# The experts of the first 16 tokens by fetched rows, the dense expert products over the other 240 tokens

## The chip, the core and the metric

The kernel runs on one NeuronCore of a Trainium2 chip. The core has TensorE (matrix products into PSUM), VectorE, ScalarE, GpSimd and SyncE, which run side by side, each through its own list of instructions in order, and wait for each other by semaphores; 16 DMA engines move data between HBM and the core's SBUF. The metric is the device time of one execution in microseconds, the median of several runs.

## The reference

A network of two layers over 256 tokens of 1024 channels, followed by a second block of another kind, all in float32. The change is in PEER, the layer of experts, which each of the two layers has. Each of 8 heads of a token picks the 16 best of 16,384 experts through two sets of 128 sub-keys; the picked experts are rows of two tables, `u_emb` and `v_emb`:

```python
q = jnp.einsum('td,dhk->thk', x_t, w_q).reshape(T, PEER_HEADS, 2, PEER_HALF)
s = jnp.einsum('thpk,hpnk->thpn', q, sub_keys).astype(jnp.float32)
sv, si = lax.top_k(s, K)
cand = (sv[:, :, 0, :, None] + sv[:, :, 1, None, :]).reshape(T, PEER_HEADS, K * K)
cidx = (si[:, :, 0, :, None] * PEER_NKEYS + si[:, :, 1, None, :]).reshape(T, PEER_HEADS, K * K)
fv, fpos = lax.top_k(cand, K)
eidx = jnp.take_along_axis(cidx, fpos, axis=-1)
gate = jax.nn.softmax(fv, axis=-1)
u = u_emb[eidx]
v = v_emb[eidx]
act = jax.nn.gelu(jnp.einsum('thkd,td->thk', u, x_t).astype(jnp.float32), approximate=False)
return jnp.einsum('thk,thkd->td', (gate * act).astype(x_t.dtype), v)
```

## The kernel before

The kernel doesn't gather. `peer` computes every expert for every token, densely: U h for all 16,384 experts, gelu, times the gate, which is zero for those not picked, and then the product with V. Both tables are streamed from HBM in 128 tiles of 128 experts (512 KB each) per layer.

All large products are made in three parts: each operand is split into a high and a low float32r part, and the product is high x high, high x low and low x high (`mm3`, and the loop in `product`). A float32r matmul is one record in the trace, a product of plain float32 is two. A tile of weights is loaded by SyncE's queue into `raw` (three places), its high part `whi` is made by ScalarE (line 88) and its low part `wlo` by VectorE (line 95), both with three places; `Stream` holds this order, and keeps three tiles split ahead of the one in use.

`peer` goes through these stages:

- Queries and scores, then **U**: for each of 128 tiles `lin_t("ut", hT)` makes one block of 128 experts by 256 tokens in 8 x 3 matmuls (line 364). The tokens `hh`, `hl` are the moving operand, so a matmul has 256 columns. During the first 64 tiles (`I0`) `Background` lets VectorE do the routing (`peer_top`, `peer_route`) in pieces: after each tile a budget of 1,450 ns of it is written into the order (`pump`), by an estimate for each piece.
- During the second 64 tiles the gates are spread by expert, in groups of four tokens: VectorE makes one-hot tiles `pm`, `qm`, ScalarE multiplies the gates in (line 967), TensorE multiplies the two (line 974), and VectorE multiplies the result into the activations `wl`, `wu` (`gates`). 64 groups cover the tokens.
- **V**: for each of 128 tiles the activations of its experts are split (`split_w`, two tiles ahead, line 984 on ScalarE, 985 on VectorE) and multiplied: 8 blocks of 128 channels by 256 tokens, three matmuls each (lines 303 to 305), summed in four PSUM banks `pss`. In layer 0, 56 steps of the modulation run beside V on VectorE (line 214), each with a load of 512 KB into one of three `sp` places.
- `turn_over` adds the result to x and makes the next stage's operand.

GpSimd has nothing to do in V. The order on every engine is the order of the Python calls; each engine waits only for the data and the places of its next instruction.

Of the kernel before, what the change touches and what calls it, by code (L numbers as in the profile page):

```python
# [43 lines left out]
class Stream:  # L44
    """Weights in the order of their use: loads and splits into two float32r parts run ahead."""
# [46 lines left out]
    def end(self):  # L92
        """The low part."""
# [26 lines left out]
class Slots:  # L120
    """A ring of given places."""
# [9 lines left out]
class Background:  # L131
    """Work that is traced between the products, by its time on VectorE."""
# [28 lines left out]
def net(ctx, tc, A, out):  # L161
# [37 lines left out]

    consts = cst.tile([128, 2], FT, name="consts")  # L200
# [17 lines left out]
    def ada_done(l, i):  # L218
        """Finish the modulation vector i of layer l: add its bias."""
# [5 lines left out]
    def ada_gain(l, i, norm):  # L225
        """(1 + scale) * gain, by channel."""
# [5 lines left out]
    def spread_row(g, dst):  # L232
        """A vector by channel [128, 8] as a row on every partition."""
# [11 lines left out]
    def gains(name):  # L245
        """Scale and shift by channel behind a norm."""
# [24 lines left out]
    def mix(main, side):  # L271
        """Spread side evenly among main, from its start."""
# [1765 lines left out]
```

## Time and profile before

| | |
|---|---|
| runs | 2477.17, 2473.5, 2476.11 us |
| median | 2476.11 us |
| profiled execution, first to last instruction | 2471.6 us |
| TensorE busy | 2416.0 us, 98% |
| VectorE busy | 1849.0 us, 75% |
| ScalarE busy | 1383.7 us, 56% |
| GpSimd busy | 18.2 us, 1% |
| U of layer 0, first to last matmul | about 168 to 590 us |
| V of layer 0 | about 592 to 955 us |
| U and V of layer 1 | about 1187 to 1609 and 1610 to 1973 us |

The profile names an instruction by its line, its engine and the tiles that it writes and reads (`pa<-gh,whi`: the accumulator `pa` from `gh` and `whi`), with partitions x elements. TensorE's matmuls overlap in the trace, so the length of a record (0.28 us for 256 columns) is not the time that it costs; the distance from one start to the next is. "PEclk" is the granted clock as a share of 2.4 GHz. A row of the timeline with "x16" is 16 records in a row, its length from the first's start to the last's end. Idle time stands behind its row in brackets with what ended it.

### The profile page before, as it was taken

How to read it: one execution, taken by the hardware profiler on the slowest of the kernel's cores; microseconds unless marked ns; L12 is line 12 of the kernel's file. 1: busy time of each engine (PE TensorE's matmuls, PEld its weight loads, DVE VectorE, ACT ScalarE, POOL GpSimd, SP SyncE). 2: the span in 40 equal slices, each digit the busy share in tenths (PEclk: the TensorE clock that was granted, in tenths of full speed). 3: DMA queues.
4: the chain of work that ended last, by engine and by line, in shares of the span. 5: the costliest groups of instructions: out<-in, count | busy, mean ns of one | idle time of the engine just before them, and what ended most of it. 6: DMA issues, size and time to landing. Idle time of an engine off the chain costs nothing. (4 is left out here: it accounts for less than half of the span.)

```text
span 2471.6 us, 49525 instructions
## 1 busy us (share of the span) xinstructions
PE 2416.0 (98%) x19700; PEld 2368.7 (96%) x19700; DVE 1849.0 (75%) x3537; ACT 1383.7 (56%) x2666; POOL 18.2 (1%) x31
## 2 busy tenths in 40 slices
PE   5999999999999999999999999999999999999998
PEld 4899999999999999889999999999999988999998
DVE  7988988897777778777888888855555676476864
ACT  4565467775454446666455777654444564455443
POOL 0000000000000000000000000000000000000000
PEclk8999999999999999999999999999999999999999
DMA  9555554446777776445555444455665552034564
GB/s 380 232 183 180 188 172 138 134 138 205 269 270 269 269 270 210 154 146 195 172 185 183 150 133 137 154 183 186 187 187 184 176 176 72 26 120 158 186 194 137
DMA packets 123640, 450.23 MB, mean 182 GB/s; under 512 B 14136, under 2 KB 15160, under 8 KB 122256
## 3 DMA queue, kind: packets, MB, share of 16 engines
q1 hardware_dynamic: 122320, 439.53, 53.4%
q0 software_dynamic: 1088, 7.54, 0.8%
q8 instruction: 154, 2.52, 0.4%
q14 instruction: 78, 0.64, 0.1%
HBM read 443.87 MB, written 3.15 MB: 181 GB/s over the span
## 5 line engine op out<-in xcount | busy, mean ns | idle before, releaser
L95 DVE TENSOR_TENSOR wlo<-raw,whi 128x1024 fp32r<-128x1024 f32 x701 | 854.4, 1220 | 253.1 <-ACT whi L88 249.9
L364 PE MATMUL pa<-hh,whi 128*128 128x256 f32 (+1 forms) x2904 | 826.1, 286 | 0.0
L364 PE MATMUL pa<-hl,whi 128*128 128x256 f32 (+1 forms) x2904 | 807.5, 281 | 0.0
L364 PE MATMUL pa<-hh,wlo 128*128 128x256 f32 (+1 forms) x2904 | 804.0, 282 | 0.9 <-DVE wlo L95 0.9
L88 ACT ACTIVATE whi<-raw 128x1024 fp32r<-128x1024 f32 x701 | 735.2, 1050 | 95.4 <-PE pa L304 50.7
L304 PE MATMUL pa<-gl,whi 128*128 128x256 f32 x2000 | 561.9, 281 | 0.0
L305 PE MATMUL pa<-gh,wlo 128*128 128x256 f32 x2000 | 561.9, 281 | 0.0
L303 PE MATMUL pa<-gh,whi 128*128 128x256 f32 x2000 | 561.9, 281 | 0.0
L364 PEld LDWEIGHTS pa<-hh,whi 128*128 128x128 f32 x2904 | 546.9, 188 | 2.4 <-issue 1.3
L364 PEld LDWEIGHTS pa<-hl,whi 128*128 128x128 f32 x2904 | 545.8, 189 | 1.0 <-DVE hl L575 0.8
L364 PEld LDWEIGHTS pa<-hh,wlo 128*128 128x128 f32 x2904 | 542.8, 189 | 1.4 <-DVE wlo L95 1.3
L303 PEld LDWEIGHTS pa<-gh,whi 128*128 128x128 f32 x2000 | 376.9, 188 | 0.0
L305 PEld LDWEIGHTS pa<-gh,wlo 128*128 128x128 f32 x2000 | 376.9, 188 | 0.0
L304 PEld LDWEIGHTS pa<-gl,whi 128*128 128x128 f32 x2000 | 376.8, 188 | 0.0
L967 ACT ACTIVATE qm<-qm,wij 128x128 f32<-128x128 f32 x512 | 163.9, 402 | 26.1 <-DVE qm L959 25.6
L984 ACT ACTIVATE gh<-wu 128x256 fp32r<-128x256 f32 x128 | 53.4, 417 | 181.1 <-PE pa L305 181.0
L984 ACT ACTIVATE gh<-wl 128x256 fp32r<-128x256 f32 x126 | 52.4, 417 | 174.9 <-PE pa L305 174.0
L946 ACT ACTIVATE wl<-pa 128x256 f32<-128x256 f32 x128 | 49.1, 383 | 152.0 <-PE pa L364 151.8
L974 PE MATMUL pb<-qm,pm 128*128 128x128 f32 x1024 | 132.4, 275 | 0.0
L974 PEld LDWEIGHTS pb<-qm,pm 128*128 128x128 f32 x1024 | 123.8, 191 | 0.0
L957 DVE TENSOR_TENSOR pm<-iota,wij 128x512 f32<-128x512 f32 x128 | 87.4, 683 | 43.8 <-PE pb L974 43.8
L985 DVE TENSOR_TENSOR gl<-wu,gh 128x256 fp32r<-128x256 f32 x128 | 54.4, 425 | 67.7 <-ACT gh L984 64.1
(546 smaller groups left out, 3107.1 us busy)
## 6 DMA issues: line engine op xcount, KB each, us to landing
raw<-in_ut_dram SPq DMA_DIRECT2D x256, 512.0 KB, 3.5
raw<-in_v_dram SPq DMA_DIRECT2D x256, 512.0 KB, 4.1
sp<-in_ada_dram SPq DMA_DIRECT2D x56, 512.0 KB, 4.8
ada<-in_ada_dram SPq DMA_DIRECT2D x40, 512.0 KB, 10.2
raw<-in_peer_q_dram SPq DMA_DIRECT2D x32, 512.0 KB, 3.9
raw<-in_up_dram SPq DMA_DIRECT2D x32, 512.0 KB, 3.6
raw<-in_down_dram SPq DMA_DIRECT2D x32, 512.0 KB, 3.5
raw<-in_od_in_dram SPq DMA_DIRECT2D x24, 512.0 KB, 4.2
```

The costliest lines, as they stand in the source:

```text
L88: self.nc.scalar.activation(hi[:, :width], t[:, :width], AF.Copy)
L95: self.nc.vector.tensor_tensor(lo, t, hi, op=OP.subtract)
L303: PE.matmul(ps, lhsT=lh, rhs=rh, start=start, stop=False)
L304: PE.matmul(ps, lhsT=lh, rhs=rl, start=False, stop=False)
L305: PE.matmul(ps, lhsT=ll, rhs=rh, start=False, stop=stop)
L364: PE.matmul(ps, lhsT=part[a], rhs=part[b], start=start and i == 0, stop=stop and i == len(names) - 1)
L946: ACT.activation(t[:, k, gtok:], ps[:, gtok:], AF.Gelu)
L957: V.tensor_tensor(pm, iota[:, None, :].to_broadcast([128, 4, 128]), wij[:, 2, t0:t0 + 4, None].to_broadcast([128, 4, 128]), op=OP.is_equal)
L967: ACT.activation(qm[:, j], qm[:, j], AF.Copy, scale=wij[:, 0, t:t + 1])
L974: PE.matmul(ps[:, j * 128:j * 128 + 128], lhsT=pm[:, j], rhs=qm[:, j], start=True, stop=True)
L984: ACT.activation(gh, t[:, k], AF.Copy)
L985: V.tensor_tensor(gl, t[:, k], gh, op=OP.subtract)
```

## The change

The first 16 tokens (`SP`) leave the dense products. Their picks are 16 tokens x 8 heads x 16 = 2,048 rows of each table; with token and head on the 128 partitions that is 16 picks per partition. `peer_route` packs gate and expert number of these tokens into `pk`, and eight small transfers on GpSimd's queue bring them to `picks` (128 partitions, 16 gates and 16 numbers). The dense U, the one-hot groups, the gates and the dense V then cover 240 tokens (`ND`), 60 groups instead of 64.

Between U and V, ScalarE copies the identity and the first 16 tokens' operand (`reps`, both parts, repeated for the 8 heads), and 16 matmuls bring these onto the partitions in two PSUM banks `htok`. The generator `sparse` does the rest beside V: 16 indirect transfers of 128 rows of 4 KB from U (512 KB each) by GpSimd, VectorE's product of each with `htok` with a sum in two halves of 512, a gelu, the gate, then 16 such transfers from V and a multiply-add each into `ysp`. It holds two places for rows in layer 0 and five in layer 1. From the fourth V tile on, each tile's budget is 450 ns in layer 0 and 900 in layer 1; a row counts 1,300. At the end 8 matmuls of 16 columns with `folds` add the heads' sums to the 16 columns of `pss` that the dense product leaves out. The modulation steps of layer 0 have two places instead of three.

```diff
+SP = 16
+ND = S - SP
@@ product
+        ps = acc(hT.w - hT.c0)[:n]
+            part = {"lh": w[0][:, cs], "ll": w[1][:, cs], "rh": hT.hh[:, k, hT.c0:hT.w],
+                    "rl": hT.hl[:, k, hT.c0:hT.w]}
@@ into
+        mm3(block(pss, c)[:, c0:], w[0][:, cs], w[1][:, cs], rh, rl, start and c % 2 == 0, stop and c % 2 == 1)
@@ peer_route
+        if b == 0:
+            pk = pool.tile([128, 8, 2, 16], FT, name="pk")
+            V.tensor_copy(pk[:SP, :, 0], gate[:SP])
+            V.scalar_tensor_tensor(pk[:SP, :, 1], sel[:SP, 0], 128.0, sel[:SP, 1], op0=OP.mult, op1=OP.add)
+            for h in range(8):
+                G.dma_start(picks[h * SP:h * SP + SP], pk[:SP, h])
@@ peer, between U and V
+            htok = [bank(), bank()]
+            identr = two.tile([128, 128], FR, name="identr")
+            ACT.activation(identr, ident, AF.Copy)
+            reps = [two.tile([128, 8, 8, SP], FR, name="reps", tag="rows", bufs=2) for _ in range(2)]
+            for rep, t in zip(reps, (hT.hh, hT.hl)):
+                ACT.activation(rep, t[:, :, None, :SP].to_broadcast([128, 8, 8, SP]), AF.Copy)
+            for k in range(8):
+                for n, rep in enumerate(reps):
+                    PE.matmul(htok[k // 4][:, k % 4 * 128:k % 4 * 128 + 128],
+                              lhsT=rep[:, k].rearrange("p h t -> p (h t)"), rhs=identr, start=n == 0, stop=n == 1)
...
+                pools["spare"] = (Slots(places[1:]), 2)
...
+            def sparse():
+                pick = two.tile([128, 16], I32, name="pick")
+                act = two.tile([128, 16], FT, name="act")
+                V.tensor_scalar(pick, picks[:, 1], float(l * 16384), None, op0=OP.add)
+                def fetch(table, k):
+                    r = rows.tile(None, FT, "rows")
+                    G.indirect_dma_start(out=r, out_offset=None, in_=A[table].rearrange("l i p d -> (l i p) d"),
+                                         in_offset=bass.IndirectOffsetOnAxis(ap=pick[:, k:k + 1], axis=0))
+                    return r
+                order = [(t, k) for t in ("u", "v") for k in range(16)]
+                ahead = len(rows.places)
+                got = [fetch(*o) for o in order[:ahead]]
+                yield 300
+                for n, (t, k) in enumerate(order):
+                    r = got.pop(0)
+                    if t == "u":
+                        hs = (slice(0, 512), slice(512, 1024))
+                        for q in range(2):
+                            V.tensor_tensor_reduce(r[:, hs[q]], r[:, hs[q]], htok[q], scale=1.0,
+                                                   scalar=act[:, k:k + 1] if q else 0.0, op0=OP.mult, op1=OP.add,
+                                                   accum_out=act[:, k:k + 1])
+                    elif k == 0:
+                        ACT.activation(act, act, AF.Gelu)
+                        V.tensor_tensor(act, act, picks[:, 0], op=OP.mult)
+                        V.tensor_scalar(ysp, r, act[:, 0:1], None, op0=OP.mult)
+                    else:
+                        V.scalar_tensor_tensor(ysp, r, act[:, k:k + 1], ysp, op0=OP.mult, op1=OP.add)
+                    if n + ahead < 32:
+                        got.append(fetch(*order[n + ahead]))
+                    yield 1300
+                for c in range(8):
+                    PE.matmul(block(pss, c)[:, :SP], lhsT=ysp[:, c * 128:c * 128 + 128], rhs=folds, start=False, stop=False)
+                yield 0
+            bg.set(sparse())
@@ the loop over V's tiles
+                if i == 120:
+                    bg.flush()
+                if i > 2:
+                    bg.pump(450 if l == 0 else 900)
                 split_w(i + 2)
                 w_ = st.next("v")
```

Two places in the order. The first is ScalarE between U and V of layer 0; `gtmp` is the gelu of U's last tiles, `wij_r` and `gh` are the high parts of the first experts' activations. Before:

```order
L88 ACTIVATE whi<-raw 128x1024
L984 ACTIVATE wij_r<-wl 128x256
L949 ACTIVATE gtmp<-pa 128x256
L984 ACTIVATE gh<-wl 128x256
L240 ACTIVATE sp<-pb 128x512 x2
L984 ACTIVATE gh<-wl 128x256
L88 ACTIVATE whi<-raw 128x1024
```

And now:

```order
L90 ACTIVATE whi<-raw 128x1024
L998 ACTIVATE wij_r<-wl 128x240
L963 ACTIVATE gtmp<-pa 128x240
L998 ACTIVATE gh<-wl 128x240
L1080 ACTIVATE identr<-ident 128x128
L1083 ACTIVATE reps<-hh 128x1024
L1083 ACTIVATE reps<-hl 128x1024
L243 ACTIVATE sp<-pb 128x512 x2
L998 ACTIVATE gh<-wl 128x240
L90 ACTIVATE whi<-raw 128x1024
```

The three copies stand behind the first `gh`. On TensorE the 16 matmuls that read them stand right behind U's last matmul, ahead of V's first.

The second place is VectorE at V's first tiles in layer 0; the line pairs `L985`/`L999` and `L95`/`L97` are the low parts of the activations and of the weights, `L214`/`L217` a modulation step. Before:

```order
L985 TENSOR_TENSOR gl<-wl,gh 128x256
L95 TENSOR_TENSOR wlo<-raw,whi 128x1024
L985 TENSOR_TENSOR gl<-wl,gh 128x256
L95 TENSOR_TENSOR wlo<-raw,whi 128x1024
L985 TENSOR_TENSOR gl<-wl,gh 128x256
L214 ISA sp,mod<-sp 128x1024
L214 ISA mod 128x1
L95 TENSOR_TENSOR wlo<-raw,whi 128x1024
```

And now:

```order
L999 TENSOR_TENSOR gl<-wl,gh 128x240
L97 TENSOR_TENSOR wlo<-raw,whi 128x1024
L1103 TENSOR_SCALAR pick<-picks 128x16
L1120 ISA rows,act<-rows,pb 128x512
L1120 ISA act 128x1
L1120 ISA rows,act<-rows,pb,act 128x512
L1120 ISA act 128x1
L999 TENSOR_TENSOR gl<-wl,gh 128x240
L217 ISA sp,mod<-sp 128x1024
L217 ISA mod 128x1
L97 TENSOR_TENSOR wlo<-raw,whi 128x1024
```

The row numbers (`pick`) and the first fetched row's product stand directly one behind the other, ahead of the next tile's `gl` and `wlo`. Later rows of the order have one such row in every third tile of layer 0.

## Rows read from the trace of the kernel before

**Rows 1.** The page: span, and its part 1, busy time by engine.

```profile
span 2471.6 us, 49525 instructions
PE 2416.0 (98%) x19700; PEld 2368.7 (96%) x19700; DVE 1849.0 (75%) x3537; ACT 1383.7 (56%) x2666; POOL 18.2 (1%) x31
```

**Rows 2.** Busy time by stretch: two of U in layer 0, V in layers 0 and 1.

```profile
core 0: us, PE busy (x) PEld busy (x) DVE busy (x) ACT busy (x) POOL busy (x), PEclk, DMA share, GB/s
230.00:300.00 70.00, 70.00 (x592) 70.00 (x591) 64.37 (x188) 35.97 (x55) 0.00 (x0) 1.00 0.60 189
250.00:350.00 100.00, 100.00 (x844) 100.00 (x843) 88.40 (x263) 53.46 (x78) 0.00 (x0) 1.00 0.58 186
700.00:800.00 100.00, 100.00 (x847) 100.00 (x847) 74.70 (x103) 48.38 (x72) 0.00 (x0) 1.00 0.76 270
1700.00:1800.00 100.00, 100.00 (x848) 100.00 (x847) 58.19 (x71) 47.91 (x70) 0.00 (x0) 1.00 0.61 186
```

**Rows 3.** Timeline of TensorE elsewhere: start us, length us, engine, line, operation, tiles, forms.

```profile
1080.57 0.39 PE L305 MATMUL pa<-whi,ml 128*128 128x512 f32 x1
1080.80 0.39 PE L303 MATMUL pa<-whi,mh 128*128 128x512 f32 x1
...
2068.23 0.28 PE L364 MATMUL pa<-hl,whi 128*32 128x256 f32 x1
2068.35 0.28 PE L364 MATMUL pa<-hh,wlo 128*32 128x256 f32 x1
...
2162.95 1.89 PE L1735 MATMUL pb<-rhs,XT 128*128 128x64 f32 x16
...
2234.07 1.89 PE L1800 MATMUL pb<-kT,qT 128*128 128x256 f32 x8
```

**Rows 4.** The page's part 5, groups: busy us, mean ns | idle before.

```profile
L95 DVE TENSOR_TENSOR wlo<-raw,whi 128x1024 fp32r<-128x1024 f32 x701 | 854.4, 1220 | 253.1 <-ACT whi L88 249.9
L88 ACT ACTIVATE whi<-raw 128x1024 fp32r<-128x1024 f32 x701 | 735.2, 1050 | 95.4 <-PE pa L304 50.7
L967 ACT ACTIVATE qm<-qm,wij 128x128 f32<-128x128 f32 x512 | 163.9, 402 | 26.1 <-DVE qm L959 25.6
L974 PE MATMUL pb<-qm,pm 128*128 128x128 f32 x1024 | 132.4, 275 | 0.0
L957 DVE TENSOR_TENSOR pm<-iota,wij 128x512 f32<-128x512 f32 x128 | 87.4, 683 | 43.8 <-PE pb L974 43.8
L985 DVE TENSOR_TENSOR gl<-wu,gh 128x256 fp32r<-128x256 f32 x128 | 54.4, 425 | 67.7 <-ACT gh L984 64.1
```

**Rows 5.** Timeline from U to V in layer 0.

```profile
590.11 0.28 PE L364 MATMUL pa<-hh,wlo 128*128 128x256 f32 x1
590.22 1.95 PE L237 MATMUL pb<-ident,csil 128*128 128x128 f32 x16
590.42 0.38 ACT L949 ACTIVATE gtmp<-pa 128x256 f32<-128x256 f32 x1 [1.21 <-PE pa L364]
...
591.29 0.42 ACT L984 ACTIVATE gh<-wl 128x256 fp32r<-128x256 f32 x1 [0.49 <-DVE wu L950]
```

**Rows 6.** Groups of VectorE in V of layer 0, 600 to 950.

```profile
L214 DVE CUSTOM_DVE_ANT_0 sp<-sp 128x1024 f32<-128x1024 f32 x56 | 68.3, 1219 | 0.0
```

**Rows 7.** Waits in V of layer 0, 600 to 950: total us, times, longest.

```profile
ACT gh L984 <- PE pa L305: 172.9, 118, 1.5
```

**Rows 8.** Stretches around the idle time at 82 us; columns as in rows 2.

```profile
82.00:87.00 5.00, 1.50 (x6) 0.59 (x4) 4.41 (x9) 1.91 (x4) 0.00 (x0) 1.00 1.02 408
87.30:90.60 3.30, 3.23 (x13) 3.06 (x14) 2.71 (x8) 2.73 (x6) 0.00 (x0) 0.50 1.02 412
```

**Rows 9.** DMA issues: queue, count, size each, median us to landing.

```profile
raw<-in_v_dram SPq DMA_DIRECT2D x256, 512.0 KB, 4.1
...
vM<-vm_dram POOLq DMA_DIRECT2D x1, 1024.0 KB, 12.1
```

**Rows 10.** Groups of GpSimd: busy us, mean ns | idle before.

```profile
L1781 POOL DMA_DIRECT2D vM<-vm_dram x1 | 0.5, 527 | 0.0
```

More of the change, by code (lines that the diff above doesn't have):

```diff
@@ L198, in col @@
         return cols[:, a + i:a + i + n]
+    folds = cst.tile([128, SP], FT, name="folds")
     consts = cst.tile([128, 2], FT, name="consts")
@@ L380, in block, with into @@
         return pss[c // 2][:, c % 2 * 256:c % 2 * 256 + 256]
-    def into(pss, c, w, rh, rl, start, stop):
+    def into(pss, c, w, rh, rl, start, stop, c0=0):
         cs = slice(c * 128, c * 128 + 128)
-        mm3(block(pss, c), w[0][:, cs], w[1][:, cs], rh, rl, start and c % 2 == 0, stop and c % 2 == 1)
+        mm3(block(pss, c)[:, c0:], w[0][:, cs], w[1][:, cs], rh, rl, start and c % 2 == 0, stop and c % 2 == 1)
     def approach(left, nxt, extra):
@@ L935, in peer @@
             low = es.enter_context(tc.tile_pool(name="low", bufs=1))
-            wl = low.tile([128, I0, 256], FT, name="wl")
+            wl = low.tile([128, I0, ND], FT, name="wl")
+            picks = low.tile([128, 2, 16], FT, name="picks")
             wij = low.tile([128, 3, 256], FT, name="wij")
@@ L944, in a_tile @@
                 t, k = tile_at(i)
-                if gtok < 256:
+                if gtok < ND:
                     ACT.activation(t[:, k, gtok:], ps[:, gtok:], AF.Gelu)
                 if gtok > 0:
-                    tmp = one.tile([128, 256], FT, name="gtmp", bufs=2)
+                    tmp = one.tile([128, ND], FT, name="gtmp", bufs=2)
                     ACT.activation(tmp[:, :gtok], ps[:, :gtok], AF.Gelu)
@@ L981, in split_w @@
                 if gh is None:
-                    gh = two.tile([128, 256], FR, name="gh", bufs=3)
-                    gl = two.tile([128, 256], FR, name="gl", bufs=3)
+                    gh = two.tile([128, ND], FR, name="gh", bufs=3)
+                    gl = two.tile([128, ND], FR, name="gl", bufs=3)
                 ACT.activation(gh, t[:, k], AF.Copy)
@@ L1023, in peer @@
             up = es.enter_context(tc.tile_pool(name="up", bufs=1))
-            wu = up.tile([128, 128 - I0, 256], FT, name="wu")
+            wu = up.tile([128, 128 - I0, ND], FT, name="wu")
             es1 = ExitStack()
@@ L1048, in peer @@
                     gated += 1
-            while spread_ < 64:
+            while spread_ < ND // 4:
                 for g in range(spread_, made):
@@ new lines, in peer @@
+            for rep, t in zip(reps, (hT.hh, hT.hl)):
[4 more added lines that the diff above has]
+                              lhsT=rep[:, k].rearrange("p h t -> p (h t)"), rhs=identr, start=n == 0, stop=n == 1)
+            sp = [hp.tile([128, 8 * 258], FT, name="sp", tag=t) for t in ("hh", "hl")]
@@ new lines, in peer @@
+            places = [sp[0][:, :1024], sp[0][:, 1024:2048], sp[1][:, :1024]]
+            ysp = sp[1][:, 1024:2048]
+            rows = [two.tile([128, 1024], FT, name="rows", tag="rows", bufs=2) for _ in range(2)]
+            if l == 0:
+                cact[0] = spread_row(csil, places[0])
+                pools["spare"] = (Slots(places[1:]), 2)
+            else:
+                rows += places
+            rows = Slots(rows)
+            def sparse():
[10 more added lines that the diff above has]
+                got = [fetch(*o) for o in order[:ahead]]
+                yield 300
+                for n, (t, k) in enumerate(order):
[10 more added lines that the diff above has]
+                        V.tensor_scalar(ysp, r, act[:, 0:1], None, op0=OP.mult)
+                    else:
+                        V.scalar_tensor_tensor(ysp, r, act[:, k:k + 1], ysp, op0=OP.mult, op1=OP.add)
[5 more added lines that the diff above has]
+                yield 0
@@ L1094, in peer @@
                 if 127 - i == 5:
-                    room = again(low, "wl", I0 // 8, 2048)
+                    room = again(low, "wl", 2, 2048)
                     extra = pairs(room[:, 0], room[:, 1])
@@ L1892, in net @@
     nc.sync.dma_start(x, A["x"])
+    V.tensor_reduce(folds, ident.rearrange("p (h t) -> p t h", t=SP), axis=AX.X, op=OP.add)
     st.load()
@@ L1971, in _layouts @@
     out["v"] = f(n["peer_v"].reshape(2, 128, 128, 1024))
+    out["u"] = f(n["peer_u"].reshape(2, 128, 128, 1024))
     od = n["od_w_in"][0]
```

26 lines of the change are left out of this document (12 added, 14 removed).

## The prediction

> **What bounds the kernel now.** I read the page's busy shares first: TensorE is busy 98% of the span, VectorE 75% [rows 1]. So the question in the experts' stages is what paces TensorE there. The stretches of 100 us say it [rows 2]: the granted clock is 1.00, the DMA engines are busy 0.58 to 0.76, and TensorE is busy 100.00 of 100.00 in the first product (U), and in the second (V) of both layers, with 844, 847 and 848 matmuls, that is 118.5 ns from one to the next in U and 118.1 in V, though one record lasts 280 ns [rows 5] (records overlap, so I count starts, never durations). VectorE in the same stretches has 88, 75 and 58 us of work per 100: near its limit in U while it also does the routing, with room in V. The table of waits for V of layer 0 has ScalarE waiting for TensorE 172.9 us of 350 [rows 7]: the work that feeds TensorE runs ahead of it. So the path here is the row of matmuls itself, and what changes their spacing or stops the row changes the time.
>
> **Part 1: 240 columns instead of 256.** 128 tiles x 8 blocks x 3 parts x 2 products x 2 layers = 12,288 matmuls get 16 columns less. What is a column worth? A single-pass matmul of 512 columns starts 0.23 us after the one before (1080.57, 1080.80), one of 256 columns 0.12 (118 by the counts) [rows 2, 3]: (230 - 118) / 256 = 0.44 ns a column, 7.0 ns for 16, so 111.3 ns. Could the weights of 128 columns, loaded for every matmul, hold the spacing at 118 whatever the columns? The products with 32 columns of weights and 256 moving ones still start 0.12 apart (2068.23, 2068.35) [rows 3]: at 256 it is the moving columns. But there is a floor further down: matmuls of 128 columns in full float32, which are two records each, follow one another 16 records in 1.95 us, and those of half the columns, 64, 16 in 1.89 us [rows 3, 5]. Less the last one's 0.28 us that is 111 and 107 ns: half the columns bring 4 ns. So something else, for a 128-column weight tile, holds the spacing at 107 to 111 ns, and 240 columns come out just at the place where the two meet. I take 111.5 ns, the upper of them, because near-equal limits add their jitter. Gain: 6,144 x (118.5 - 111.5) + 6,144 x (118.1 - 111.5) = 43.0 + 40.6 = 83.6 us. Bounds: 107 ns gives 138 us, 118 gives nothing.
> The Trainium skill (TensorE: Matmul & The Clock Gate, LDWEIGHTS and Back-to-back issue gap) gives 106.7 ns for loading 128 columns and N/2.4 + 2.5 ns from one warm matmul to the next, 109.2 at 256 and 102.5 at 240 columns; this trace has 118, not 109.2, at 256. By the page's load time the product would take 106.7 ns, the gain would be 142 us and the time, estimated, 2355 us; the measured spacing decides, and the sum goes without it.
>
> **Part 2: what TensorE is spared and given beside.** 60 groups of tokens are spread by one-hot products instead of 64: the line has 1,024 records for 64 groups x 4 tokens x 2 records x 2 layers [rows 4], so 64 records go, at 0.111 us 7.1 us. It gets 16 matmuls that bring the first tokens' rows in front of V, and 8 full-float32 ones (16 records) that fold the result, in each layer: 64 records, 7.1 us. They cancel.
>
> **Part 3: the step from U to V.** Today TensorE goes on without a pause: U's last matmul starts at 590.11, the next work at 590.22 [rows 5]. In the changed kernel the 16 matmuls stand there, and they need two copies of 128 x 1024 and one of 128 x 128 that ScalarE makes. These stand in its order behind the gelu of the last U tile (590.42) and the split that waits for VectorE's product with it (591.29, 0.42) [rows 5], so they can't begin before 591.7; a copy of 128 x 128 takes 0.40 and one of 128 x 1024 1.05 us [rows 4]. The second large one ends at 591.7 + 0.4 + 2 x 1.05 = 594.2, 4.0 us after TensorE ran dry. Nothing covers it, since TensorE's order is fixed: 2 x 4.0 = 8.0 us. Idle time has a second price here: after 3.5 idle us of the five from 82 on (busy 1.50 of 5.00) the granted clock was 0.50 for the next 3.3 us, 1.2 instead of 2.4 GHz [rows 8]. I add half of 3.4 us twice, 3.4 us; the bounds are 0 and, for idle and clock, 11.4 together.
>
> **Part 4: the start of the rows' work.** At V's fourth tile VectorE's order gets the row numbers (a 128 x 16 operation) and right behind it the first product with a fetched row, which nothing can have fetched before. VectorE stands for the whole fetch, and behind it in its queue stand the split of the second operand's tile 5, in layer 0 a modulation step, and the low part of weight tile 5. TensorE then has the rest of tile 2 (0.5 us) and tiles 3 and 4 (2 x 2.68): 5.9 us. After the fetch VectorE needs two 512-wide products (0.68 each), 0.43, 1.22 (layer 0) and 1.22 us [rows 4, 6], 4.2 us, or 3.0 in layer 1. With a fetch of L the stop is L - 1.7 and L - 2.9. No indirect transfer is in this trace. Nearest below: 512 KB of V on SP's queue land in 4.1 us. Nearest above: the second of GpSimd's two transfers of 1 MB, issued together, lands in 12.1 [rows 9]. I take L = 6, half of the latter, as it is GpSimd's queue: 4.3 + 3.1 = 7.4 us; the bounds give 4 to 20.
>
> **Part 5: VectorE and the queues under the shorter tile.** A tile of 24 matmuls is 2.84 us now and 2.68 after. While VectorE routes it has 64.37 of 70 us, 92% [rows 2], or 97% of the shorter tile: mostly hidden by the two tiles that are split ahead, I take 2 us for both layers (0 to 10). In V of layer 0 it has 74.70 per 100, 2.12 us a tile. A row's work is 1.36 us for a row of U and 1.22 for one of V, by the nearest rows; 1,300 are counted for 450 a tile, so 0.35 of a row a tile, 0.45 us: 2.57 of 2.68. In layer 1 it is 1.64 + 0.69 x 1.3 = 2.54. So VectorE stays under TensorE, and I cost it at nothing; the cover is 0.1 us a tile, and if it is gone the price is in the second case below. DMA: 16.8 MB in layer 0 over 93 tiles of 2.68 us are 67 GB/s on top of 270 x 2.84 / 2.68 = 286: 353, where another stretch had 412 [rows 2, 8]. SP's loads wait behind nothing new, since the rows go by GpSimd's queue, which has nothing else in V.
>
> **Sum.** -83.6 - 7.1 + 7.1 + 8.0 + 3.4 + 7.4 + 2.0 = -62.8 us. The profiled span is 2471.6 [rows 1] and becomes 2409; the median of the three runs, 2476.1, is 4.5 above that span, and becomes 2413.
>
> **The rivals.** (a) VectorE becomes the bound in V of layer 0. A tile there has 0.11 us to spare, and a fetch for every third tile must block VectorE by only 0.3 us to use that up. GpSimd is busy 0.53 us with a plain transfer [rows 10]; if VectorE stands for so long, the tile is 0.53 x 0.35 - 0.11 = 0.08 us late, 93 tiles 7 us; if an indirect one holds it 1.5 us, 0.41 and 39 us. Time 2420 to 2452. For it: VectorE's many two-operand work; against: layer 1 has the same margin only for half as many tiles, and no row here shows the two engines in each other's way. The Trainium skill (SBUF — State Buffer, Who interferes with whom) says just this, that a VectorE instruction with two SBUF inputs and a GpSimd instruction that reads SBUF exclude each other for their whole length; no run here shows it yet.
> (b) Slower: the rows come too late. In layer 1 a row is due every 1,300 / 900 = 1.44 tiles, 3.9 us, and VectorE waits in order. GpSimd's queue brought 2 MB in 12.1 us [rows 9], 3.0 for 512 KB, which suffices. If each row takes 5.8 us instead, 32 x (5.8 - 3.9) = 61 us are lost and the gain is gone; from there on the kernel is slower. At 8 us a row it is 32 x 4.1 in layer 1 and, where one is due every 7.7, 32 x 0.3 in layer 0: 141 us, 2554.
> (c) The change doesn't do what it says, because narrower matmuls aren't faster: at 118 ns for 240 columns the sum is +20.8, 2497. No single-pass matmul under 256 columns is in this trace. The far end is the two-record form, 8 records of 256 columns in 1.89 us [rows 3], 216 each and 432 a product: if 240 columns fell to that, 12,288 x 0.29 us would be added, about 6000 us. Against: order and counts of instructions stay, only the count of columns changes.
>
> **How the numbers follow.** Forecast 0.62; the same with spacings below 110 ns 0.04; (a) 0.16; (b) 0.10; (c) 0.05 at 2497 and 0.03 at the far end. The predicted time is the forecast's, 2413. Its own range is 2388 (110 ns) to 2440 (113 ns, a fetch of 12 us). To leave out no more than 2 in 10 the range goes on over (a) and to (c)'s first value: 2388 to 2500; left out are most of (b), the far end and the smallest spacings. About 0.2% (5 us) is what a measurement of this kernel can tell from no change. Faster by more: 0.62 + 0.04 + 0.16, less the forecast's and (a)'s outermost cases, 0.80. Within: 0.04, the early part of (b). Slower: 0.16.
>
> **What would show it.** 100 us of V should hold some 895 matmuls and a tile 2.68 us; 847 mean (c). Between U and V TensorE should stand 4 us, ScalarE's two copies ending it, with a dip of the granted clock behind; and some 3 to 4 us at V's sixth tile, ended by VectorE's low part. In V of layer 0 VectorE should be above 90%; if TensorE's idle time there is ended by VectorE all along, (a) holds, and if VectorE's own waits name the rows' DMA after the first, (b). The forecast is wrong if the spacing is off by 2 ns, which is 25 us, or if one wait repeats with every row.

## The result, and the profile after

The changed kernel takes 2446.24 us (median of 4 runs, 2442.92 to 2449.18) against 2475.42 before: a ratio of 0.988, 95% interval 0.9866 to 0.9894. It is faster by 29 us, where 62.8 were forecast. The sign and the range held; more than half of the gain is missing. The profiled execution took 2447.65 us, its span is 2445.9 against 2471.6 [rows 1].

The busy shares of the page say little by themselves. TensorE, VectorE and GpSimd after:

```profile
span 2445.9 us, 49822 instructions
PE 2367.2 (97%) x19700; PEld 2314.2 (95%) x19700; DVE 1900.5 (78%) x3674; ACT 1374.9 (56%) x2635; POOL 119.6 (5%) x111
```

TensorE has the same 19,700 records as before and 48.8 us less busy time, but the span is only 25.7 us shorter: some 23 us of new idle time stand against the gain. The busy time by stretch (columns as in rows 2) says where. The first three lines are U in layer 0, V in layer 0 while rows are fetched, V in layer 1 when all of its rows are done; the next four lie right behind U and at V's first tiles, in layer 0 and in layer 1. The last three are V while rows are worked off: layer 0, then layer 1 in a stretch that all runs can be compared in, and the part of that stretch in which rows are still fetched (the last fetch is issued at 1710).

```profile
250.00:350.00 100.00, 100.00 (x883) 100.00 (x883) 90.05 (x261) 56.98 (x89) 0.00 (x0) 1.00 0.62 194
700.00:800.00 100.00, 97.79 (x855) 96.56 (x855) 86.99 (x127) 51.80 (x76) 17.34 (x13) 1.00 0.93 334
1740.00:1840.00 100.00, 100.00 (x891) 100.00 (x891) 60.45 (x74) 50.24 (x75) 0.00 (x0) 1.00 0.63 195
...
574.60:581.40 6.80, 6.80 (x34) 6.80 (x33) 0.00 (x0) 1.39 (x4) 0.00 (x0) 0.50 0.18 66
598.50:605.30 6.80, 5.75 (x27) 5.76 (x28) 6.65 (x12) 0.40 (x1) 0.74 (x2) 0.50 0.77 270
1584.90:1591.70 6.80, 6.17 (x29) 6.05 (x29) 1.96 (x3) 2.23 (x4) 0.00 (x0) 0.50 0.27 83
1608.90:1612.20 3.30, 3.30 (x18) 3.30 (x17) 3.30 (x5) 0.41 (x1) 1.99 (x1) 0.50 0.98 386
...
606.00:850.00 244.00, 239.01 (x2088) 236.06 (x2087) 212.22 (x331) 123.00 (x180) 41.36 (x29) 1.00 0.93 332
1613.00:1740.00 127.00, 124.79 (x1099) 124.00 (x1099) 104.79 (x162) 63.54 (x92) 38.73 (x26) 1.00 0.85 298
1613.00:1710.00 97.00, 95.46 (x841) 94.86 (x840) 81.60 (x135) 48.83 (x71) 36.61 (x24) 1.00 0.90 319
```

Counted as the prediction counted, U has 883 matmuls in 100 us, 113.3 ns from one to the next, and V 891, 112.2 ns, where no rows come. (A count takes in the two or three records that still run at the window's start; the mean from start to start is 0.3 to 0.4 ns longer, 112.5 in V, and the expectations below go by that.) Where they come in layer 0 there are 855: TensorE stands there although its clock is granted in full, with the DMA engines busy 0.93 of the time.

Two stops are plain in the timeline. From U to V of layer 0 (U's last matmul starts at 570.35):

```profile
570.66 0.37 ACT L963 ACTIVATE gtmp<-pa 128x240 f32<-128x240 f32 x1 [1.11 <-PE pa L369]
...
571.50 0.40 ACT L998 ACTIVATE gh<-wl 128x240 fp32r<-128x240 f32 x1 [0.47 <-DVE wu L964]
571.81 0.29 ACT L1080 ACTIVATE identr<-ident 128x128 fp32r<-128x128 f32 x1
...
572.01 1.04 ACT L1083 ACTIVATE reps<-hh 128x1024 fp32r<-128x1024 f32 x1
...
572.96 1.05 ACT L1083 ACTIVATE reps<-hl 128x1024 fp32r<-128x1024 f32 x1
...
573.11 0.33 PE L1086 MATMUL pb<-identr,reps 128*128 128x128 f32 x1 [2.49 <-ACT reps L1083]
...
574.06 2.99 PE L1086 MATMUL pb<-identr,reps 128*128 128x128 f32 x15 [0.62 <-ACT reps L1083]
```

This is the step that the prediction laid out, with the instructions in its order: TensorE stands 2.49 + 0.62 = 3.1 us. From 574.6 on its granted clock is 0.50, 1.2 instead of 2.4 GHz, for 6.8 us, though it is busy throughout. In layer 1 it stands 2.49 + 0.63 us, and the same stretch follows. At V's first tiles, 588 to 600 us:

```profile
588.99 0.17 DVE L1103 TENSOR_SCALAR pick<-picks 128x16 int32<-128x16 f32 x1
...
590.12 1.01 POOL L1107 DMA_INDIRECT rows<-in_u_dram,pick  x1 [341.91 <-ACT gh L998]
...
595.40 0.69 DVE L1120 CUSTOM_DVE_ANT_0 rows<-rows,pb 128x512 f32<-128x512 f32 x1 [6.25 <-DMA rows<-in_u_dram,pick]
...
596.81 0.41 DVE L999 TENSOR_TENSOR gl<-wl,gh 128x240 fp32r<-128x240 f32 x1
...
597.27 0.38 PE L307 MATMUL pa<-gl,whi 128*128 128x240 f32 x1 [2.64 <-DVE gl L999]
598.27 0.08 DVE L217 DVE_READ_ACCUMULATOR2_ANT mod<- 128x1 f32 x1
598.27 1.22 DVE L97 TENSOR_TENSOR wlo<-raw,whi 128x1024 fp32r<-128x1024 f32 x1
...
599.54 0.57 PE L308 MATMUL pa<-gh,wlo 128*128 128x240 f32 x1 [1.90 <-DVE wlo L97]
```

VectorE stands 6.25 us for the first row, and TensorE 2.64 us for the low part queued behind it and 1.90 us more for the next. A second stretch of 6.8 us at half clock follows from 598.5. In layer 1 TensorE stands 2.27 + 0.76 us here, and the stretch is 3.4 us long.

The third loss isn't one stop but many small ones. In the table of waits for V of layer 0, 606 to 850 us (total us, times, longest), ScalarE waits for raw weight tiles. Before, then after:

```profile
ACT whi L88 <- DMA raw<-in_v_dram: 0.2, 1, 0.2
```

```profile
ACT whi L90 <- DMA raw<-in_v_dram: 80.3, 51, 4.7
```

To compare runs I read five lengths from the timeline: U from ScalarE's first gelu to its last, the step from there to V's first matmul, and V from its first matmul to its last (us, layer 0 / layer 1). The lengths are of one execution each; the kernel before, run again beside each set of experiments, took 2474.35 to 2475.6 us:

| kernel | time | ratio to before, 95% | U | step | V |
|---|---|---|---|---|---|
| before | 2475.42 | | 419.8 / 419.8 | 1.5 / -0.2 | 363.6 / 363.8 |
| changed | 2446.24 | 0.9866 to 0.9894 | 400.2 / 400.2 | 9.6 / 6.7 | 365.3 / 357.4 |
| 240 columns alone | 2406.47 | 0.9706 to 0.9738 | 400.9 / 400.2 | 1.5 / -0.2 | 347.4 / 347.7 |
| 248 columns alone | 2427.36 | 0.9787 to 0.982 | 406.5 / 406.5 | 1.5 / -0.2 | 351.5 / 351.6 |
| 224 columns alone | 2383.35 | 0.9617 to 0.965 | 392.3 / 392.3 | 1.5 / -0.2 | 344.8 / 345.1 |
| rows fetched, hardly worked on | 2436.83 | 0.9831 to 0.9864 | 400.1 / 400.1 | 9.7 / 6.7 | 358.4 / 353.3 |
| rows worked on, not fetched | 2434.79 | 0.9822 to 0.9855 | 400.2 / 400.2 | 9.4 / 6.4 | 356.0 / 355.5 |
| products behind V's first tile | 2433.91 | 0.9809 to 0.9844 | 400.2 / 400.1 | 1.5 / -0.2 | 364.8 / 359.6 |
| first fetches early | 2432.30 | 0.981 to 0.9845 | 400.2 / 400.2 | 10.0 / 5.7 | 357.4 / 350.2 |
| both moves | 2422.73 | 0.9763 to 0.9799 | 400.1 / 400.2 | 1.5 / -0.2 | 359.6 / 355.3 |
| both, 450 a tile in both layers | 2418.63 | 0.9756 to 0.9793 | 400.2 / 400.2 | 1.5 / -0.2 | 356.2 / 350.5 |
| the same at 370 a tile | 2419.44 | 0.976 to 0.9794 | 400.1 / 400.2 | 1.5 / -0.2 | 361.3 / 349.9 |
| at 450, no modulation transfers | 2409.81 | 0.9722 to 0.9754 | 400.2 / 400.1 | 1.5 / -0.2 | 350.0 / 350.0 |
| at 450, plain transfers | 2417.17 | 0.9748 to 0.978 | 400.1 / 400.2 | 1.5 / -0.2 | 360.4 / 350.0 |

U wins 19.6 us in each layer; V of layer 0 is 1.7 us longer than before and V of layer 1 6.4 us shorter. The theory to test: the narrower matmul brings about 69 us; what is missing goes to the two stops with their stretches of half clock, and to transfers of rows that make weight tiles late. The rival is the first of the prediction's: VectorE, or GpSimd in VectorE's way, paces V.

### The profile page after: what moved, and what is told of

It reads as the page before. It is cut to its first block, busy times and chain, and to the rows that moved or that the text cites. A ratio compares the mean times of both kernels' runs of the same rounds, so it can differ in the third digit from the quotient of the medians.

```text
span 2445.9 us, 49822 instructions
## 1 busy us (share of the span) xinstructions
PE 2367.2 (97%) x19700; PEld 2314.2 (95%) x19700; DVE 1900.5 (78%) x3674; ACT 1374.9 (56%) x2635; POOL 119.6 (5%) x111
## 5 line engine op out<-in xcount | busy, mean ns | idle before, releaser
L97 DVE TENSOR_TENSOR wlo<-raw,whi 128x1024 fp32r<-128x1024 f32 x701 | 855.1, 1221 | 257.6 <-ACT whi L90 251.9
L369 PE MATMUL pa<-hh,whi 128*128 128x240 f32 (+2 forms) x2904 | 818.7, 284 | 0.4 <-ACT hh L578 0.4
L369 PE MATMUL pa<-hh,wlo 128*128 128x240 f32 (+2 forms) x2904 | 793.3, 278 | 1.7 <-DVE wlo L97 1.7
L369 PE MATMUL pa<-hl,whi 128*128 128x240 f32 (+2 forms) x2904 | 793.8, 277 | 0.0
L308 PE MATMUL pa<-gh,wlo 128*128 128x240 f32 x2000 | 556.0, 278 | 9.0 <-DVE wlo L97 8.8
L307 PE MATMUL pa<-gl,whi 128*128 128x240 f32 x2000 | 553.0, 276 | 4.9 <-DVE gl L999 2.6
L306 PE MATMUL pa<-gh,whi 128*128 128x240 f32 x2000 | 553.7, 277 | 0.8 <-ACT whi L90 0.8
L960 ACT ACTIVATE wl<-pa 128x240 f32<-128x240 f32 x128 | 47.3, 370 | 135.2 <-PE pa L369 135.0
L998 ACT ACTIVATE gh<-wu 128x240 fp32r<-128x240 f32 x128 | 51.4, 401 | 119.3 <-PE pa L308 119.2
L998 ACT ACTIVATE gh<-wl 128x240 fp32r<-128x240 f32 x126 | 49.8, 395 | 65.1 <-PE pa L308 59.9
L999 DVE TENSOR_TENSOR gl<-wu,gh 128x240 fp32r<-128x240 f32 x128 | 52.1, 407 | 40.8 <-ACT gh L998 40.7
```

What stands on the lines that cost most here:

```text
L97: self.nc.vector.tensor_tensor(lo, t, hi, op=OP.subtract)
L306: PE.matmul(ps, lhsT=lh, rhs=rh, start=start, stop=False)
L307: PE.matmul(ps, lhsT=lh, rhs=rl, start=False, stop=False)
L308: PE.matmul(ps, lhsT=ll, rhs=rh, start=False, stop=stop)
L369: PE.matmul(ps, lhsT=part[a], rhs=part[b], start=start and i == 0, stop=stop and i == len(names) - 1)
L960: ACT.activation(t[:, k, gtok:], ps[:, gtok:], AF.Gelu)
```

## Experiments: the narrower products alone

The work on the first 16 tokens is taken out; zeros go through the folds.

```diff
-            htok = [bank(), bank()]           # with its copies and 16 products
             def sparse():
+                G.memset(ysp, 0.0)            # no pick, no fetch, no product with a row
```

> The narrower products alone: the experts of the first 16 tokens are left out (no rows are fetched, nothing is worked on them, no product brings their tokens in front of V; zeros go through the folds). The part of the change that was to gain. If a matmul of 240 columns costs what the changed kernel shows in its clean stretches, 113.3 ns in U and 112.5 in V, it gives 6,144 x 5.4 + 6,144 x 5.8 = 69 us, and the sixteen spread and fold records of a layer about 3 more: 2475 - 72 = 2403 us. If the 111.5 ns of the prediction hold and the rows slow even the clean stretches, 2475 - 87 = 2388. If U's 113.3 ns come from VectorE rather than from TensorE, U stays at 400 us and V falls below 343.

Measured 2406.47 us, 68 us less than before. So the columns give what the changed kernel's clean stretches say, and U is the same 400 us: the rows cost nothing in U. VectorE's routing (89 to 90 us of 100) hardly stops TensorE under the shorter tile: from start to start U has 113.6 ns in its first half, with the routing, and 113.2 in its second, without, and only in this run one layer took 0.7 us more. What the rows add is 2446 - 2406 = 40 us.

Is 112 ns a floor? The same with 224 and with 248 columns, by one number:

```diff
-C0 = 16
+C0 = 32
```

> As the run of 240 columns alone, with 224 columns (the first 32 tokens' experts left out). If the moving columns set the spacing (0.44 ns each), V falls from 112.5 to 105.4 ns a matmul, both products together by 87 us: about 2313 us. If 112 ns is a floor for a weight tile of 128 columns, V's spacing stays at 110 to 112 and the gain is the 4 spread groups fewer in each layer, 7 us, and up to 25 us from the spacing: 2370 to 2396.

> The narrower products alone, with 248 columns (the first 8 tokens' experts left out). At 256 columns V has 118.3 ns a matmul, at 240 112.5, at 224 111.7. If columns cost 0.44 ns each down to a floor of 111.5 to 112.5, 248 gives 114.8 ns and the time is 2475 - 12,288 x 3.5 = 2432 us less 3 for two spread groups fewer in each layer: 2429. If the slope between 256 and 240 is even (0.36 ns a column), 115.4 and 2436.

V of layer 0, 700 to 800 us, with 240, then 224, then 248 columns, and a stretch of U for the last (columns as in rows 2):

```profile
700.00:800.00 100.00, 100.00 (x892) 100.00 (x891) 78.34 (x109) 50.49 (x74) 0.00 (x0) 1.00 0.83 285
```

```profile
700.00:800.00 100.00, 100.00 (x898) 100.00 (x897) 77.30 (x108) 51.53 (x75) 0.00 (x0) 1.00 0.84 283
```

```profile
250.00:350.00 100.00, 100.00 (x872) 100.00 (x871) 91.11 (x269) 55.16 (x81) 2.05 (x5) 1.00 0.64 193
700.00:800.00 100.00, 100.00 (x882) 100.00 (x881) 77.05 (x107) 50.41 (x74) 0.00 (x0) 1.00 0.81 280
```

With the 847 of 256 columns [rows 2] the spacings are 118.1, 113.4, 112.1 and 111.4 ns for 256, 248, 240 and 224. From 240 to 224 columns 0.7 ns are won, not 7: a floor, and the prediction's place for it, 111 ns, is right to 1 ns in V. What the forecast and both cases of the expectation for 248 had wrong is the way to it: the first 8 columns bring 4.7 ns, the next 8 only 1.3. The run of 248 came out 2 us under the expected 2429; from start to start U has 115.0 ns, near the expected 114.8, and V 113.7, 1.1 shorter.

## Experiments: the transfers or VectorE

First the fetches without the work: VectorE reads one column of each row.

```diff
-V.tensor_tensor_reduce(r[:, hs[q]], r[:, hs[q]], htok[q], ...)     # two halves
+V.tensor_scalar(act[:, k:k + 1], r[:, 0:1], 1.0, None, op0=OP.mult)
-V.scalar_tensor_tensor(ysp, r, act[:, k:k + 1], ysp, ...)
+V.scalar_tensor_tensor(ysp[:, :1], r[:, :1], act[:, k:k + 1], ysp[:, :1], ...)
```

> The changed kernel, every row fetched as there, but VectorE's products with the rows left out (it reads one column of each row, so the pace and the order of fetches stay; one full row's product per layer is kept). Of VectorE's 44 us of row work a layer, nearly all goes. If V is slowed by the rows' transfers, which keep the weight tiles from arriving, V of layer 0 stays at 362 to 366 us and ScalarE's waits for raw weight tiles stay near 120 us: 2440 to 2447 us. If V is slowed by VectorE being full, V of layer 0 falls to 350 us or less and V of layer 1 to 352: 2425 us.

Then the work without the fetches:

```diff
 def fetch(table, k):
     r = rows.tile(None, FT, "rows")
+    if not (table == "u" and k < ahead):
+        return r
     G.indirect_dma_start(out=r, ...)
...
-V.tensor_tensor_reduce(r[:, hs[q]], r[:, hs[q]], htok[q], ...)
+V.tensor_tensor_reduce(ysp[:, hs[q]], r[:, hs[q]], htok[q], ...)   # so that the rows stay
```

> The changed kernel with all of VectorE's row work, but only the first rows of a layer fetched (2 in layer 0, 5 in layer 1); the later products read these again. If the rows' transfers slow V, V of layer 0 falls from 365 to about 350 us and V of layer 1 from 357 to 352 (what is left over 24 x 126 x 112.5 is the stop at V's first tiles), ScalarE's waits for raw tiles all but vanish: about 2426 us. If VectorE's load slows V, V stays at 362 to 366 and the time at 2440 to 2447.

Fetched but hardly worked on, 2436.83 us, between the two cases that were expected: V of layer 0 still takes 11 us more than with no rows, some 5 of them in the stretch below (2,126 matmuls against 2,171) and most of the rest at the stop at V's first tiles (1.41 + 1.90 us idle, then 3.4 us at half clock). Worked on but not fetched, 2434.79, again between the two cases (2426, and 2440 to 2447). The stretch 606 to 850 us of the two, fetches alone first:

```profile
606.00:850.00 244.00, 241.64 (x2126) 239.81 (x2124) 186.09 (x298) 125.65 (x184) 38.93 (x28) 1.00 0.94 339
```

```profile
606.00:850.00 244.00, 244.00 (x2170) 244.00 (x2169) 222.11 (x343) 129.21 (x187) 0.00 (x0) 1.00 0.83 281
...
1613.00:1740.00 127.00, 127.00 (x1132) 127.00 (x1130) 105.92 (x154) 62.69 (x94) 0.00 (x0) 1.00 0.64 194
```

Without transfers VectorE has more work done in this stretch than in the changed kernel (222.11 against 212.22 us, 91%) and TensorE has no idle time at all, 2,170 matmuls instead of 2,088. With the transfers and a VectorE at 76% it has idle time. So the transfers stop TensorE, and a full VectorE only makes a late tile dearer. V of layer 0 lost 9.3 us to them and V of layer 1 1.9 (365.3 - 356.0 and 357.4 - 355.5). In layer 1 the loss is larger than that: the 33 matmuls missing from 1613 to 1740 us (1,099 against 1,132) are 3.7 us, but the half clock behind the first row lasted 6.8 us without the transfers and 3.4 in the changed kernel, which hides 1.7 of them. What stays above the narrower products alone, 8.6 and 7.8 us, is the stop at V's first tiles, which this kernel still has.

GpSimd in VectorE's way would show as longer low parts, VectorE's most frequent instruction with two operands from SBUF. Groups of VectorE from 640 to 830 us, changed kernel, then without fetches:

```profile
L97 DVE TENSOR_TENSOR wlo<-raw,whi 128x1024 fp32r<-128x1024 f32 x68 | 83.2, 1223 | 22.6 <-ACT whi L90 21.2 <-issue 1.3
```

```profile
L97 DVE TENSOR_TENSOR wlo<-raw,whi 128x1024 fp32r<-128x1024 f32 x71 | 86.8, 1223 | 10.1 <-ACT whi L90 9.7
```

1,223 ns in both, and the idle time ahead of it is ended by ScalarE, which waits for the raw tile. GpSimd, though, does wait for VectorE. Two fetches of the changed kernel, one behind the start of a modulation step (both its operands lie in SBUF) and one not:

```profile
615.66 1.22 DVE L217 CUSTOM_DVE_ANT_0 sp<-sp 128x1024 f32<-128x1024 f32 x1
615.69 2.00 POOL L1107 DMA_INDIRECT rows<-in_u_dram,pick  x1 [9.41 <-DVE act L1120]
...
623.39 0.40 DVE L999 TENSOR_TENSOR gl<-wl,gh 128x240 fp32r<-128x240 f32 x1
623.74 0.94 POOL L1107 DMA_INDIRECT rows<-in_u_dram,pick  x1 [6.05 <-DVE act L1120]
```

Of the 64 fetches 33 began while a low part of weights or a modulation step ran, and 31 of these kept GpSimd busy for 1.8 to 2.3 us; the 31 others took 0.93 to 1.07. In the two left over the fetch took 0.94 us and the low part 1.28 instead of 1.22. The Trainium skill (SBUF — State Buffer, Who interferes with whom) says that a VectorE instruction with two SBUF inputs and a GpSimd instruction that reads SBUF exclude each other. The trace agrees, but nearly all of the waiting is GpSimd's, about 1.06 us a fetch, and VectorE loses at most 0.07 us in a fetch. So this doesn't pace V.

## Experiments: the two stops

The 16 products move behind V's first tile; ScalarE's copies stay.

```diff
-            for k in range(8):                 # the 16 products, now in first_tokens()
...
-            bg.set(sparse())
...
+                if i == 0:                     # at the end of V's first tile
+                    gen = sparse(first_tokens())
+                    bg.set(gen)
```

> The changed kernel with one move: the 16 matmuls that bring the first tokens' rows stand behind V's first tile instead of ahead of it (ScalarE's copies stay where they are). If TensorE's idle time between U and V is what these copies cost, the step from U to V falls from 9.6 and 6.7 us by 3.1 idle us and by the 3.4 us lost in 6.8 us at half clock: 2 x 6.5 = 13 us less than the changed kernel, 2433, and no granted clock of 0.50 right behind U. If another feeder is as late (V's own first operands on ScalarE, which stands behind its copies), V's first tiles wait instead and less than 4 us are won: above 2442.

The row numbers and the first fetches go ahead of V's first tile:

```diff
-            bg.set(sparse())
+            gen = sparse()
+            next(gen)                          # pick and the first fetches
+            bg.set(gen)
-                if i > 2:
+                if i > 4:
                     bg.pump(450 if l == 0 else 900)
```

> The changed kernel with the row numbers and the first fetches of a layer issued ahead of V's first tile, and the first product with a row two tiles later, so that VectorE finds it there. If VectorE's stand at the first row stops TensorE (2.64 + 1.90 us in layer 0, 2.27 + 0.76 in layer 1, then 6.8 and 3.4 us at half clock), all of it goes: 4.5 + 3.4 + 3.0 + 1.7 = 12.6 us, 2434 us. If the stop comes from the fetches' load on the DMA queues, it moves to where they now lie and the time stays within 4 us of the changed kernel's 2446.

Both, with the fetches right behind the moved products and the first row one tile later still:

```diff
                 if i == 0:
                     gen = sparse(first_tokens())
+                    next(gen)
                     bg.set(gen)
...
-                if i > 2:
+                if i > 5:
```

> Both moves together. If the two stops are independent, their gains add: 2446 - 13 - 12.6 = 2420 us, and what then lies above the narrower products alone (2406) is the work of 16 and 8 matmuls per layer, 7 us, and what the rows' transfers cost, some 11. If the half-clock stretch is moved rather than removed, 2428 or more.

2433.91, 2432.30 and 2422.73 us: each move wins 12 to 14 us and both 23.5, 3 short of their sum. The steps of 9.6 and 6.7 us fall to those of before in the first. Around the start of V in layer 0, 565 to 610 us, first the products moved, then the fetches, then both:

```profile
565.00:610.00 45.00, 40.16 (x342) 39.78 (x341) 28.09 (x54) 20.52 (x33) 4.91 (x4) 0.96 0.70 235
```

```profile
565.00:610.00 45.00, 41.89 (x342) 41.55 (x341) 29.84 (x57) 21.33 (x34) 4.92 (x4) 0.92 0.74 245
```

```profile
565.00:610.00 45.00, 44.24 (x393) 44.05 (x392) 34.68 (x66) 23.67 (x37) 7.42 (x5) 1.00 0.78 270
```

With one stop left the mean clock is 0.96 or 0.92, with none 1.00: the half clock belonged to the stops and went with them.

## Experiments: rate, form and neighbours of the transfers

Both moves, and layer 1 at layer 0's pace:

```diff
-                    bg.pump(450 if l == 0 else 900)
+                    bg.pump(450)
```

> Both moves, and layer 1 works its rows off at layer 0's pace (450 a tile instead of 900), over twice as many tiles. If the stalls in layer 1 come from the transfers' rate (0.85 DMA share, 298 GB/s where rows come in layer 1, 0.64 without), they vanish at half the rate, some 260 GB/s: 2 us less than with both moves, 2418. If each row costs a stall of its own, whatever the rate, the time is that of both moves. If a low part of VectorE's queue is what a row delays, it is 2 us more.

2418.63 us, the fastest version of the change: 57 us less than before, 27.6 less than the change as it was made. V of layer 0 and rows of layer 1, both stretches:

```profile
606.00:850.00 244.00, 241.00 (x2120) 239.18 (x2120) 215.92 (x332) 124.27 (x182) 41.10 (x28) 1.00 0.94 338
...
1613.00:1740.00 127.00, 127.00 (x1131) 127.00 (x1131) 95.56 (x147) 65.12 (x96) 19.12 (x17) 1.00 0.81 262
```

The kernel with both moves, which differs in layer 1's pace alone, while its rows come in layer 1:

```profile
1587.00:1694.00 107.00, 104.46 (x912) 103.14 (x912) 90.39 (x151) 52.87 (x77) 38.45 (x26) 1.00 0.91 318
```

In layer 1 the same rows, at 262 instead of 318 GB/s, cost nothing: 1,131 matmuls in 127 us and no idle time, as without rows, where at the faster pace TensorE had 2.5 us of idle time in 107. V of layer 1 falls from 355.3 to 350.5 us. (The 298 GB/s of the expectation are a mean with 30 us in which no row is fetched any more; while rows came it was 319.) It isn't the row but the rate. In layer 0 the modulation's 56 transfers lie beside the rows. Without them (and with VectorE's later sums scaled down, in the same instruction):

```diff
-            self.nc.sync.dma_start(t[:, :width], ap)
+            if src != "spare" or self.first < 2:
+                self.nc.sync.dma_start(t[:, :width], ap)
+                self.first += src == "spare"
```

> Both moves and 450 a tile, but of the 56 transfers of 512 KB for the modulation in V of layer 0 only the first two are made; VectorE's work on them stays, so the modulation vectors of layer 1 are left out. VectorE, ScalarE, GpSimd and TensorE do the same work as with both moves and 450 a tile. If the sum of the transfers stalls V of layer 0, 84 GB/s less (some 250 in all) puts it where layer 1 is: V falls from 356 to 350.5 us, ScalarE's waits for raw tiles from 89 to under 25 us, the time from 2418.6 to 2413. If an indirect fetch hurts by itself, next to VectorE's fuller queue in layer 0, V stays at 355 to 357.

```profile
606.00:850.00 244.00, 244.00 (x2171) 244.00 (x2170) 221.84 (x339) 127.58 (x186) 44.12 (x28) 1.00 0.78 258
```

And ScalarE's wait for raw tiles in the same stretch, then that of the kernel at 450 with the modulation:

```profile
ACT whi L92 <- DMA raw<-in_v_dram: 19.3, 21, 1.7
```

```profile
ACT whi L90 <- DMA raw<-in_v_dram: 86.7, 59, 2.9
```

2409.81 us against an expected 2413: V takes 350.0 us in both layers, with every fetch and all of VectorE's, ScalarE's and GpSimd's work in place. The modulation's transfers alone stop nothing either (no rows fetched: 281 GB/s, 2,170 matmuls). This settles the cause: the sum of what is transferred. Whether the 16 DMA engines, HBM or the place of the modulation's loads in SyncE's queue sets the limit, no run tells apart. Is it also the form of the fetch? Plain transfers of the same size:

```diff
-G.indirect_dma_start(out=r, ..., in_offset=bass.IndirectOffsetOnAxis(ap=pick[:, k:k + 1], axis=0))
+G.dma_start(r, A[table][l, k])
```

> Both moves and 450 a tile, every indirect fetch replaced by a plain transfer of the same 512 KB in one piece from the same table, on the same queue (so the rows are not those that were picked). If it is the bytes that stall V of layer 0, it stays at 354 to 357 us and the time at 2418. If it is the fetch by row (GpSimd 1.5 us busy with each instead of 0.5, 128 places in memory), V of layer 0 falls to 350 and the time to 2413.

2417.17 us, the same within the intervals, and V of layer 0 no shorter, though each transfer keeps GpSimd busy for only about a third as long. GpSimd's groups here, and with fetches by row:

```profile
L1107 POOL DMA_DIRECT2D rows<-in_v_dram x23 | 12.2, 530 | 172.9 <-DVE sp L1127 126.2 <-DVE act L1119 29.7 <-DVE sp L1125 16.9
```

```profile
L1107 POOL DMA_INDIRECT rows<-in_v_dram,pick x23 | 34.3, 1491 | 146.2 <-DVE sp L1128 96.1 <-DVE act L1120 24.8 <-DVE sp L1126 12.9
```

Last, layer 0's rows over more tiles:

```diff
-                    bg.pump(450)
+                    bg.pump(370)
```

> Both moves, and the rows spread over nearly all of V's tiles in both layers (370 a tile, 112 tiles). In layer 0 the weights and the modulation rows take 282 GB/s, the rows at 450 a tile some 60 more, in 93 tiles. If TensorE's stalls there depend on the rate near the DMA engines' limit, 330 instead of 342 GB/s wins part of what is left in V of layer 0 (356 against 347 us without rows): 3 us, 2415. If they grow with the number of tiles in which rows come, V of layer 0 takes 358 and the time is 2420.

The first case missed: 2419.44 us instead of 2415, and in the profiled run V of layer 0 took 361.3 us, not 353. The second case has the time (2420) and not the length (358). It has to be read with care: the two kernels that differ in layer 1 alone have 359.6 and 356.2 in layer 0, so one execution at these rates says no more than 3 or 4 us. That a little less rate doesn't help there is what the runs show (325 GB/s from 606 to 850 us); how the loss depends on the rate between 258 and 325 GB/s in layer 0 is open.

## Why the forecast was right in sign and wrong in size

Three terms make up the difference: the spacing of the matmuls (15.6 us too good), the transfers (11 us, forecast at nothing) and the half clock (8.5 us too little).

| term | forecast | measured | from |
|---|---|---|---|
| narrower matmuls | -83.6 | -68 | 6,144 x (118.5 - 113.3) + 6,144 x (118.1 - 112.2), counts of the stretches |
| spread, tokens, folds | 0 | 0 | not told apart |
| idle from U to V | 8.0 | 6.2 | 2 x 3.1, timeline |
| idle at the first row | 7.4 | 7.6 | 2.64 + 1.90, and in layer 1 2.3 + 0.8 |
| half clock behind the stops | 3.4 | 11.9 | half of 6.8 + 6.8 + 6.8 + 3.4; up to 0.8 of it lies in idle time counted above |
| routing | 2.0 | 0 | no stop in U; its halves with and without routing differ by 0.4 ns, which is in the first term |
| VectorE in V | 0 | 0 | work without fetches |
| transfers in V | 0 | 11 | 2446.2 - 2434.8; 13 by the matmuls missing in both layers |
| sum | -62.8 | -31 | measured -29 |

**What bounds the kernel** held: where the row of matmuls runs, its spacing sets the time; every microsecond missing is one in which it stood or ran at half clock.

**Part 1** had the mechanism right, a floor near which 240 columns come out, and the size off: 112.2 ns in V and 113.3 in U instead of 111.5, 15 us in all, 11 of them in U. It was the 25 us for 2 ns that the prediction named as its weak place. Why U's spacing stays 1.1 ns above V's isn't settled; U has it without any rows too, and 0.7 of it in its second half, where nothing is routed. The ends of the range don't follow from what stands beside them: 110 ns gives 2395, not 2388, and 113 ns with a fetch of 12 us 2443, not 2440.

**Parts 3 and 4** had both stops at their place, with the right engine ending each. The idle time came to 13.8 us where 15.4 were forecast, and the assumed 6 us for a fetch was good: VectorE stood 6.25. The step that failed here is the clock's. It was charged once a layer, 3.4 us in all, behind the first stop only, from the dip of 3.3 us in the trace of before [rows 8]. It came behind each of the four stops, 6.8 us long behind three of them: some 11.9 us.

**Part 5** failed where it put the transfers at nothing because 353 GB/s is less than the 412 of another stretch [rows 8]. Their sum came to 332 over the rows' stretch, and TensorE lost 9 us there; in layer 1 it lost some 4 at 319. A rate that the DMA engines reach somewhere doesn't say that each tile lands in time. The row that says it is ScalarE's wait for raw tiles: next to nothing before, 80 us of 244 after. With three raw tiles and three split ones ahead some of that is still covered: 19.3 us of such waits, without the modulation's transfers, stopped nothing. VectorE at 87%, with a row's 1.4 us between two tiles, makes up less of the rest: with hardly any row work, at 76%, the loss was 5 us instead of 9. The sentence on SP's queue, that its loads wait behind nothing new, was true of the queue and not of the engines behind it. The Trainium skill (DMA: Bandwidth & Descriptors, Where 436 GB/s comes from) gives some 358 GB/s as what binds a core's transfers from HBM, and by that figure a forecast of 353 would have had next to no room. The trace doesn't agree for a short stretch, the 412 of rows 8 over 3.3 us; over 244 us no run here had more than 339.

**The rivals.** (a) gives the right time, 2420 to 2452, by the wrong mechanism: GpSimd and VectorE do exclude each other, but GpSimd waits, the low parts took 1,223 ns with and without fetches, and without transfers VectorE's full load costs nothing. (b) didn't come: behind the first row VectorE's waits from 606 to 850 us name no row. (c) is refuted by 891 matmuls in 100 us. The true case, weight tiles made late by the rows' transfers, was among none of them.

**What would show it** named 895 matmuls per 100 us (891 where no rows come, 855 where they do), 4 us between U and V with a dip (3.1 us, and a longer dip), and 3 to 4 us at V's sixth tile ended by VectorE's low part (2.64 + 1.90). VectorE above 90% in V of layer 0 was not seen: 87%, since it waits for the tiles too.

## What to carry to other kernels

When a change adds transfers beside a stream that loads its operands just ahead of use, don't compare rates: find the row for the engine that takes the tiles, see how long it already waits for them and how many it has ahead, and spread the new transfers over the stretches with the lowest DMA share; here the same rows cost nothing at shares of 0.78 and 0.81 and 4 to 9 us a layer at 0.90 and 0.93. Take the share over the time in which the transfers come, not over a longer one. Count a stop of TensorE like these (3.0 to 4.5 idle us) twice, once as idle time and once as the stretch of half clock behind it, for every stop; and remove it by moving the waiting instruction behind work that is ready and by issuing the first fetch earlier, which here won 23.5 us with the same work in another order.

## What the runs showed of the hardware

- The spacing of single-pass matmuls with a weight tile of 128 columns isn't a straight line above its floor: 118.1, 113.4, 112.1 and 111.4 ns for 256, 248, 240 and 224 moving columns. Most of the gain was there with 8 columns less.
- Two idle stretches of 2.49 and 0.62 us, with one matmul between them, were followed by 6.8 us at a granted clock of 0.50 in seven of the eight cases (four kernels, both layers), and by 3.4 us in the eighth. Stops of 1.41 + 1.90 us (rows hardly worked on, layer 0) were followed by 3.4 us, and of 1.05 + 0.76 us (the same, layer 1) by none.
- A fetch of 128 rows of 4 KB by row number keeps GpSimd busy for 0.94 us, and for 2.00 us when a VectorE instruction of 128x1024 with two operands in SBUF has begun just before; a plain transfer of the same bytes takes it 0.53 us. V of layer 0 was no shorter with plain transfers (360.4 against 356.2 us).
